# A hybrid decoder block on one core: 512-wide value rows, joined MoBA value products, gathers in every second expert pair, and an earlier overflow check

## The chip, the cores and the metric

The kernel runs on one NeuronCore of one Trainium2 chip, as one program that is launched once. The metric is the device time of an execution in microseconds (us), and a kernel's time is the median of its runs. TensorE (PE) multiplies matrices into PSUM, which has eight banks here; ScalarE (ACT), VectorE (DVE) and GpSimd (POOL) work on rows, and SyncE (SP) issues the DMAs.

## What is computed

One layer for 512 tokens of width 1024: a mixer with two branches, cross-attention into 256 memory rows, a mixture of experts, and a last RMSNorm. Cut to what matters here:

```python
def reference(x, mem, ...):
    x = x + mixer(rmsnorm(x, g_mix), ...)              # h @ w_in -> GLA q,k,v,... | MoBA q,k,v | gates
    x = x + memory_attention(rmsnorm(x, g_cross), ...) # 4 heads, 256 memory rows
    x = x + hier_moe(rmsnorm(x, g_moe), ...)           # top-1 of 4 groups, top-2 of its 8 experts
    return rmsnorm(x, g_final)

# MoBA, 8 heads of 64: softmax over the own block and chosen past blocks, then
#   out = p_own @ v_own + p_sel @ v_sel
# expert e on its tokens xb, with routing weight w:
#   hid = silu(xb @ w_gate[e]) * (xb @ w_up[e]);  y = (hid @ w_down[e]) * w
```

All numbers are float32. The gate, up and down weights of the 32 experts (1024x512, 1024x512 and 512x1024 each) are 201 MB of the 252 MB that the kernel moves.

## The kernel before, in words

**Front.** The weights of the projections, output and memory stages come through SP's queue as tiles of 512 KB (`wraw`). Each is split into a high and a low part (`wsplit`: ACT copies `whi`, DVE or POOL subtracts for `wlo`), and a product is three matmuls (`mm3`). Two forms exist: `in_feat` puts features on the partitions and has 512 tokens as columns (PSUM tile `fo`), and `in_rows` puts 128 tokens on the partitions and a strip of the weight's columns beside them (tiles `ro0` to `ro3`). `in_rows` makes the values: `vg` for GLA, `vm` for MoBA and `vc` for the memory, each in two passes of 256 columns. At the very start the rows of `x` are normalised (`rms_scale` squares them, by default on ACT, for `x_in[1]` on DVE), transposed and split (`to_feat`: `hTh` by ACT, `hTl` by DVE).

**MoBA.** For four head pairs (`hp`) and four query tiles (`i`) the kernel forms scores (`s_ps`), normalises them on DVE and ACT (`pr`), transposes them (`ptp`) into `pt`, and multiplies by the values (`mo_ps`). The program is software-pipelined by one item: the value products of an item stand behind the scores of the next one. Between the scores and the transposes of an item, `weave` puts matmuls of the gates (`fo`) as filling; how many is set by the table `FILL`.

**Experts.** Tokens are routed to 64 places (`CAP`) for each expert; two experts make a pair, and there are 16 pairs p = 0 to 15. A group is two pairs. `gather` collects the tokens of a group into `xT` by a product with one-hot rows (tile `g_ps`, eight steps); `gate_up` makes `gu_ps` in eight k steps; `hidden` and `hidden_t` give `hid_t` (tile `ht_ps`); `down` makes `y_ps`; `combine` adds a pair's result to `x` during the next pair (tile `c_ps`, eight steps). `c_bcast` (tile `cb_ps`, four steps) spreads codes and routing weights over the partitions before the first combination. Each pair needs 24 weight tiles of 512 KB (`we`), 16 for gate and up and 8 for down. `eload(n)` issues them in the order of use until n are issued: `DEPTH` tiles ahead of the pair's own first, `D0` for pair 0. All lie in a pool of 48 buffers that the front's tiles share, at most 8 DMAs are outstanding, and a DMA whose buffer isn't free holds SP's queue.

**Overflow.** An expert with more than 64 tokens is finished in a loop (`overflow`) whose count `n_extra` is read from the device (`values_load`, a TENSOR_LOAD on each engine). With these inputs it runs no turn: the page of the profile has 128 loads each of gate, up and down, no more than the pairs need. Every engine passes the loop's entry, and no `eload` past `elimit` is made ahead of it. The order within a pair is that of the code: gate and up, hidden, combine and gather steps, down.

Of the kernel before, what the change touches and what calls it, by code (L numbers as in the profile page):

```python
# [70 lines left out]
def block_kernel(ctx, tc, x, mem, g_mem, rel_bias, g_mix, w_in, w_alpha_up, b_alpha, g_gla_head, w_proj_gla,  # L71
# [94 lines left out]
    def chain(*gens):  # L166
        for g in gens:
            yield from g

# [20 lines left out]
    for j in range(2):  # L190
        add_rows(w_in, 512 + 256 * j, 256)
    add_feat(w_in, 2064, 4)
    add_feat(w_in, 1552, 4)
    for j in range(2):
        add_rows(w_in, 2576 + 256 * j, 256)
# [9 lines left out]
    for j in range(2):  # L205
        add_rows(w_ckv, 512 + 256 * j, 256)
# [152 lines left out]
    def in_rows(n, evac, src, nt=NT, mark=None):  # L359
        acc = [ps(f"ro{t}", [n]) for t in range(nt)]  # L360
        for kh in range(2):
            wh, wl = wnext(4, n)
            for t in range(nt):
                for k in range(4):
                    kk = 4 * kh + k
                    mm3(acc[t], src.hi[kk][:, tcol(t)], src.lo[kk][:, tcol(t)], wh[:, k, :], wl[:, k, :], kk == 0,
                        kk == KD - 1)
                    yield 0.33
                if kh:
                    evac(t, acc[t])  # L370
        marks.add(mark)
# [107 lines left out]
    def project():  # L479
        yield from in_feat(2, lambda i, o: S.activation(qk[2 + i], o, AF.Copy), hT)  # L480
        yield from in_feat(2, lambda i, o: S.activation(qk[i], o, AF.Copy, scale=0.125), hT, mark="qk")
        for j in range(2):
            yield from in_rows(256, lambda t, o: S.activation(vg[t][:, 256 * j:256 * j + 256], o, AF.Copy), hT)
        marks.add("v")
        yield from in_feat(4, keys, hT)
        yield from in_feat(4, queries, hT)
        vm.extend(rows2("vm", NT))
        for j in range(2):
            yield from in_rows(256, lambda t, o: S.activation(vm[t][:, 256 * j:256 * j + 256], o, AF.Copy), hT)
# [148 lines left out]
    def moba():  # L638
        def scores(hp, i):
            L = (i + 1) * P  # L640
            far = max(i - 1, 0) * P
            res = []
            for half in range(2):
                h = 2 * hp + half
                s_ps = ps("s_ps", [max(L, 256)])
                for part in range(2):
                    mm(s_ps, qmT[h][:, tcol(i)], kmT[h][part][:, 0:max(L, 256)], part == 0, part == 1)
                s_ps = s_ps[:, 0:L]
                pr = med("pr", [512])
# [24 lines left out]
        def transposed(i, res):  # L674
            pts = []
            for pr, _ in res:
# [5 lines left out]
                pts.append(pt)  # L682
            return pts

        def values(hp, i, pts, o_ps):
            for j in range(i + 1):
# [7 lines left out]
        prev, o_ps = None, {}  # L694

        def finish(hp, i, pts):
            if i == 0:
                o_ps[hp] = ps("mo_ps", [T])
            values(hp, i, pts, o_ps[hp])
            if i == NT - 1:  # L700
                split(om.hi[hp], om.lo[hp], o_ps[hp])

        for hp, i in items:
            res = scores(hp, i)
            if prev:
                finish(*prev)
            yield 0.64 * FILL[i][0]
            normalise(i, res)
            yield 0.64 * FILL[i][1]
            prev = hp, i, transposed(i, res)  # L710
        yield 1.0
        finish(*prev)
# [238 lines left out]
    eloads, elimit = [0], [12 * (NE - 2) + SPILL_AT]  # L951
# [128 lines left out]
    vgen = chain(*(in_rows(256, lambda t, o, j=j: S.activation(vc[:, t, 256 * j:256 * j + 256], o, AF.Copy), mn, nt=2)  # L1080
                   for j in range(2)))
# [4 lines left out]
    steps(vgen, 16)  # L1086
# [108 lines left out]
    def gather(oh, xT, ns):  # L1195

        for k in range(KD):
            o = ps("g_ps", [ns])
# [33 lines left out]
    def hidden_t(hid, n=P):  # L1232
        t_ps = ps("ht_ps", [4, n])
# [21 lines left out]
    def combine(ot, ys):  # L1255

        for t in range(NT):
            for c, y in ys.items():
                o = ps("c_ps", [512])
# [5 lines left out]
    def overflow(xi, xb):  # L1265
        n_extra = nc.values_load(xi[0:1, 0:1], min_val=0, max_val=NX - 1,
                                 skip_runtime_bounds_check_because="2 T assignments fill fewer than NX whole blocks")
        with tc.For_i(0, n_extra, 1, iteration_sync='staggered') as i:  # L1268
# [13 lines left out]
            drain(gather(oh, xT, CAP))  # L1282
            ot, ws = slot_rows(codes[0:CAP], CAP, oa)
            to = [blk("we", [2, 512]) for q in range(4)]
            gu, load = [ps("gu_ps", [512]) for q in range(2)], load_gate_up(bass.ds(e, 1), to)
# [4 lines left out]
            hid_t = hidden_t(hidden(gu, ws, CAP, hid), CAP)  # L1290
            y_ps, load = [ps("y_ps", [512]) for c in range(2)], load_down(bass.ds(e, 1), to)
# [3 lines left out]
            for c in range(2):  # L1295
                drain(combine(ot, {c: rows_hilo(y_ps[c], CAP, parts)}))

    NP = NE // 2
    bcast, slot, spill = c_bcast(), None, spill_list()
    comb, gat = iter(()), iter(())  # L1300
    xT_next = None
    for p in range(NP):
        w = blocks[2 * p:2 * p + 2]
        used = 24 * p
        if p == NP - 1:
            eload(elimit[0])
            overflow(*spilled)
            elimit[0] = 12 * NE
        eload(used + D0[0] if p == 0 else used + DEPTH)
# [4 lines left out]
        for k in range(KD):  # L1314
            gate_up(gu, k, [xT[k][:, s0 + CAP * i:s0 + CAP * i + CAP] for i in range(2)], w)
            if k % 2:
                eload(D0[1 + k // 2] if p == 0 else used + DEPTH + 2 * (k + 1))
            if p == 0 and k >= BC_AT:
                next(bcast, None)
                if k == BC_AT + 3:  # L1320
                    slot = slot_rows(sid[:, 0:1])
                    oh_next = group_hots(1)
        if p % 2 == 0 and p + 2 < NP:
# [13 lines left out]
        drain(comb)  # L1337
# [3 lines left out]
        if p % 2 and p + 3 < NP:  # L1341
            oh_next = group_hots((p + 3) // 2)
# [5 lines left out]
        for ft in range(4):  # L1348
            down(y_ps, hid_t, ft, w)
            eload(used + DEPTH + 16 + 2 * (ft + 1))  # L1350
# [34 lines left out]
    def finish(t, r):  # L1385
# [4 lines left out]
        SY.dma_start(out[tcol(t), 0:512], xg[t])  # L1390
# [21 lines left out]
SPILL_AT = 8  # L1412
# [8 lines left out]
DEPTH = 30  # L1421
D0 = 34, 37, 41, 44, 47
# [31 lines left out]
```

## Time and profile before

| | |
|---|---|
| median of 3 runs | 985.21 us (985.02 to 985.25) |
| the profiled execution | 985.1 us, its span 983.3 us |
| mean granted TensorE clock | 0.995 |
| PE busy | 961.1 us, 98% of the span |
| moved by DMA | 252.52 MB, mean 257 GB/s |

The span is what the trace covers; 1.8 us lie around it. A busy PE says little here: matmuls are pipelined, and an engine that executes one short matmul after the other is as busy as one at its peak. Stretches and gaps are read from the timeline, where a row is a run of like instructions, its first number the start and its second the time until the last of them ended. The trace counts an unsplit float32 matmul as two instructions, so a pair's gate and up products are 64 of them and its down products 32.

### The profile page before, as it was taken

What the parts mean: (1) busy time and instruction counts of PE and PEld (TensorE: products, weight loads), DVE (VectorE), ACT (ScalarE), POOL (GpSimd) and SP (SyncE); (2) the same over time, 40 slices, a digit from 0 to 9 for tenths busy, and PEclk for the clock granted to TensorE, in tenths of its full rate; (3) what the DMA queues carried; (4) which work ended last, traced back from release to release, by engine and by line L of the source; (5) the groups of instructions that cost most, each with busy time, mean ns of one, the idle gap of its engine ahead of it and who ended that gap; (6) DMA issues with size and microseconds to landing.
All of it is one profiled execution on the core that took longest, in us unless ns stands there. A gap on an engine that the chain in (4) does not pass through costs nothing. (4 is left out here: it accounts for less than half of the span.)

```text
span 983.3 us, 13899 instructions
## 1 busy us (share of the span) xinstructions
PE 961.1 (98%) x5305; PEld 645.5 (66%) x5305; DVE 474.8 (48%) x1048; ACT 311.7 (32%) x631; POOL 32.7 (3%) x46
## 2 busy tenths in 40 slices
PE   9999999999999999999999999999999999999985
PEld 7889779888788888999844555544555554455432
DVE  6343863345555746566752543434453333444314
ACT  5452633445446424455521111111111111111003
POOL 3200010000000000000000000000000000000003
PEclk9999999999999999999999999999999999999998
DMA  9512347133133522644588999999999999999993
GB/s 300 160 44 58 71 65 193 44 86 86 60 133 129 176 81 67 198 190 196 200 331 329 409 408 409 409 409 408 409 409 409 409 408 409 409 409 409 409 383 148
DMA packets 117161, 252.52 MB, mean 257 GB/s; under 512 B 10310, under 2 KB 61795, under 8 KB 117092
## 3 DMA queue, kind: packets, MB, share of 16 engines
q1 hardware_dynamic: 117092, 251.60, 69.3%
q8 instruction: 43, 0.70, 0.3%
q14 instruction: 26, 0.21, 0.1%
HBM read 247.90 MB, written 3.67 MB: 256 GB/s over the span
## 5 line engine op out<-in xcount | busy, mean ns | idle before, releaser
L136 PE MATMUL gu_ps<-we,xT 128*64 128x512 f32 x1024 | 229.3, 597 | 5.1 <-PEq L1268 3.8
L136 PEld LDWEIGHTS gu_ps<-we,xT 128*64 128x64 f32 x1024 | 78.0, 138 | 150.5 <-issue 134.6
L213 DVE TENSOR_TENSOR wlo<-wraw,whi 128x1024 fp32r<-128x1024 f32 (+1 forms) x71 | 86.6, 1238 | 90.0 <-ACT whi L212 89.8
L136 PE MATMUL y_ps<-we,hid_t 128*64 128x512 f32 x512 | 114.2, 595 | 0.3 <-issue 0.3
L1229 DVE SCALAR_TENSOR_TENSOR hid<-hid,ws,gu_ps 128x512 f32<-128x512 f32 x16 | 11.9, 747 | 194.9 <-PE gu_ps L136 194.9
L1262 DVE TENSOR_TENSOR x<-c_ps,x 128x512 f32<-128x512 f32 x120 | 76.7, 685 | 38.9 <-PE c_ps L136 38.9
L131 PE MATMUL fo<-hTh,whi 128*128 128x512 f32 x224 | 90.5, 404 | 0.0
L133 PE MATMUL fo<-hTh,wlo 128*128 128x512 f32 x224 | 87.5, 391 | 0.0
L132 PE MATMUL fo<-hTl,whi 128*128 128x512 f32 x224 | 87.4, 390 | 0.0
L136 PEld LDWEIGHTS y_ps<-we,hid_t 128*64 128x64 f32 x512 | 36.3, 137 | 68.8 <-issue 55.7
L212 ACT ACTIVATE whi<-wraw 128x1024 fp32r<-128x1024 f32 (+2 forms) x73 | 74.5, 1043 | 1.9 <-DMA wraw<-in_w_in_dram 1.8
L1228 ACT ACTIVATE hid<-gu_ps 128x512 f32<-128x512 f32 x16 | 9.6, 597 | 197.5 <-PE gu_ps L136 197.5
L136 PE MATMUL g_ps<-oh,xrh 128*128 128x256 f32 x256 | 64.6, 293 | 1.7 <-DVE oh L1030 1.7
L136 PE MATMUL g_ps<-oh,xrl 128*128 128x256 f32 x256 | 61.6, 281 | 0.0
L136 PEld LDWEIGHTS g_ps<-oh,xrh 128*128 128x128 f32 x256 | 47.0, 189 | 14.9 <-PE gu_ps L136 9.7
L133 PE MATMUL ro<-whi,hTl 128*128 128x256 f32 (+1 forms) x192 | 55.4, 289 | 0.8 <-DVE hTl L333 0.8
L131 PE MATMUL ro<-whi,hTh 128*128 128x256 f32 (+1 forms) x192 | 56.0, 291 | 0.0
L132 PE MATMUL ro<-wlo,hTh 128*128 128x256 f32 (+1 forms) x192 | 55.5, 289 | 0.2 <-POOL wlo L213 0.2
L212 ACT ACTIVATE yh<-y_ps 128x512 fp32r<-128x512 f32 x32 | 19.1, 598 | 109.9 <-PE y_ps L136 109.9
L136 PE MATMUL c_ps<-yh,ot 128*128 128x512 f32 x128 | 50.8, 397 | 0.7 <-ACT yh L212 0.7
L136 PE MATMUL c_ps<-yl,ot 128*128 128x512 f32 x128 | 50.8, 397 | 0.2 <-DVE yl L213 0.2
L131 PEld LDWEIGHTS fo<-hTh,whi 128*128 128x128 f32 x224 | 42.0, 188 | 12.0 <-issue 3.9
(320 smaller groups left out, 1544.5 us busy)
## 6 DMA issues: line engine op xcount, KB each, us to landing
we<-in_w_exp_gate_dram SPq DMA_DIRECT2D x128, 512.0 KB, 10.2
we<-in_w_exp_up_dram SPq DMA_DIRECT2D x128, 512.0 KB, 10.2
we<-in_w_exp_down_dram SPq DMA_DIRECT2D x128, 512.0 KB, 10.2
wraw<-in_w_in_dram SPq DMA_DIRECT2D x38, 512.0 KB, 3.8
wraw<-in_w_out_dram SPq DMA_DIRECT2D x8, 512.0 KB, 6.1
wraw<-in_w_ckv_dram SPq DMA_DIRECT2D x8, 512.0 KB, 4.6
wraw<-in_w_proj_gla_dram SPq DMA_DIRECT2D x4, 512.0 KB, 3.9
wraw<-in_w_proj_moba_dram SPq DMA_DIRECT2D x4, 512.0 KB, 4.3
```

The costliest lines, as they stand in the source:

```text
L131: PE.matmul(o, lh, rh, start=first, stop=False)
L132: PE.matmul(o, lh, rl, start=False, stop=False)
L133: PE.matmul(o, ll, rh, start=False, stop=last)
L136: PE.matmul(o, l, r, start=first, stop=last, **kw)
L212: S.activation(hi, src, AF.Copy)
L213: eng.tensor_tensor(lo, src, f(hi), op=ALU.subtract)
L1228: S.activation(row, gu[0][0:n], AF.Silu)
L1229: V.scalar_tensor_tensor(row, row, ws[:, 0:1], gu[1][0:n], op0=ALU.mult, op1=ALU.mult)
L1262: V.tensor_tensor(xs, o, xs, op=ALU.add)
```

## The change

1. `in_rows` makes 512 columns in one pass (two k rows to a weight tile, table `WIDE`), for `vg`, `vm` and `vc`.
2. MoBA: the transposes of a head pair's four query tiles are collected in `pa` and `pb`, copied by ACT in two pieces for tiles 2 and 3, and `values` runs once for a head pair, behind the scores of the next pair's first tile.
3. The square of `x_in[1]` is made on ACT, between the halves of `to_feat`.
4. The gather of a group stands wholly in the odd pair ahead of it (eight steps in pairs 1, 3, ... 13), not in halves in two pairs; pair 0 has none. Two of the four `c_bcast` steps stand ahead of `c_weights`. The prefetch depth is 35 tiles for pair 0 and 33 then, where it was 34 to 47 by a table and 30.
5. The overflow loop stands in pair 14 ahead of gate step k = 4, not ahead of pair 15; until there 350 tiles may be issued, not 368. Its count is loaded ahead of pair 13.
6. Four of the eight output DMAs are issued by ACT, not by SP.

```diff
-    def in_rows(n, evac, src, nt=NT, mark=None):
-        acc = [ps(f"ro{t}", [n]) for t in range(nt)]
-        for kh in range(2):
-            wh, wl = wnext(4, n)
+    def in_rows(evac, src, nt=NT, mark=None):
+        acc = [ps(f"ro{t}", [512]) for t in range(nt)]
+        kk = 0
+        for kn in WIDE:
+            wh, wl = wnext(kn, 512)
             for t in range(nt):
-                for k in range(4):
-                    kk = 4 * kh + k
-                    mm3(acc[t], src.hi[kk][:, tcol(t)], src.lo[kk][:, tcol(t)], wh[:, k, :], wl[:, k, :], kk == 0,
-                        kk == KD - 1)
-                    yield 0.33
+                for k in range(kk, kk + kn):
+                    mm3(acc[t], src.hi[k][:, tcol(t)], src.lo[k][:, tcol(t)], wh[:, k - kk, :], wl[:, k - kk, :], k == 0,
+                        k == KD - 1)
+                    yield 0.65
...
-    r1 = rms_scale(x_in[1], V)
-    to_feat(xr, hT, 0, lambda: wsplit(2))
-    rows[1] = scaled_rows(x_in[1], r1, gmix)
+    r1 = []
+    def between():
+        r1.append(rms_scale(x_in[1]))
+        wsplit(2)
+    to_feat(xr, hT, 0, between)
+    rows[1] = scaled_rows(x_in[1], r1[0], gmix)
...
-                pt = med("pt", [i + 1, P])
-                S.activation(pt, t_ps, AF.Copy)
+                n = min(i + 1, 2)
+                S.activation(pa[:, 0:n, tcol(i)], t_ps[:, 0:n, :], AF.Copy)
+                if i > 1:
+                    S.activation(pb[:, 0:i - 1, tcol(i - 2)], t_ps[:, 2:i + 1, :], AF.Copy)
...
-                    mm(o_ps[sl, tcol(i)], vm[j][:, h * 64:(h + 1) * 64], pts[half][:, j, :], j == 0, j == i,
-                       skip_group_check=True)
+                    p_j = pa[:, j, j * P:] if j < 2 else pb[:, j - 2, (j - 2) * P:]
+                    mm(o_ps[sl, j * P:], vm[j][:, h * 64:(h + 1) * 64], p_j, j == 0, j == NT - 1, skip_group_check=True)
...
-            if prev:
-                finish(*prev)
+            if prev and i == 0:
+                values(*prev)
...
-        if p == NP - 1:
-            eload(elimit[0])
-            overflow(*spilled)
-            elimit[0] = 12 * NE
-        eload(used + D0[0] if p == 0 else used + DEPTH)
+        depth = DEPTH[min(p, 1)]
+        if p == SPILL[0] - 1:
+            n_extra = nc.values_load(spilled[0][0:1, 0:1], ...)
+        eload(used + depth)
...
         for k in range(KD):
+            if (p, k) == SPILL[0:2]:
+                overflow(n_extra, *spilled)
+                elimit[0] = 12 * NE
             gate_up(gu, k, ...)
             if k % 2:
-                eload(D0[1 + k // 2] if p == 0 else used + DEPTH + 2 * (k + 1))
+                eload(used + depth + 2 * (k + 1))
...
-        if p % 2 == 0 and p + 2 < NP:
+        if p % 2 and p + 1 < NP:
             xT_next = rows2("xT", KD, 4 * CAP)
             gat = gather(oh_next, xT_next, 4 * CAP)
...
-        gs = 4 if p + 2 < NP else 0
-        steps(gat, min(gs, 1))
-        steps(comb, 2 if gs else 4)
+        steps(gat, 2)
+        steps(comb, 2 if p % 2 and p + 1 < NP else 4)
         hid_t = hidden_t(hid)
         for i in range(3):
-            steps(gat, min(gs, 1))
+            steps(gat, 2)
             steps(comb, 2)
...
-        SY.dma_start(out[tcol(t), 0:512], xg[t])
+        S.dma_start(out[tcol(t), 0:512], xg[t])
...
+WIDE = 2, 2, 2, 2
+SPILL = 14, 4, 350
-DEPTH = 30
-D0 = 34, 37, 41, 44, 47
+DEPTH = 35, 33
+OH_AT = 3
```

On PE, this is the passage from the first head pair of MoBA to the second in the program of before; `ptp` are the transposes of the last query tile, `s_ps` the scores of the next head pair's first tile, and `fo` the gates' filling:

```order
L679 MATMUL ptp<-keep,pr 128x128 x8
L136 MATMUL s_ps<-km_1092,qm_1412 128x256 x2
L136 MATMUL s_ps<-km_1093,qm_1412 128x256 x2
L136 MATMUL mo_ps<-pt,vm_1518 64x128 x4
L136 MATMUL mo_ps<-pt,vm_1519 64x128 x4
L131 MATMUL fo<-hTh_145,whi 128x512
```

and this is the same passage in the program of the change:

```order
L675 MATMUL ptp<-keep,pr 128x128 x8
L136 MATMUL s_ps<-km_989,qm_1309 128x256 x2
L136 MATMUL s_ps<-km_990,qm_1309 128x256 x2
L136 MATMUL mo_ps<-pa,vm_1415 64x512 x2
L136 MATMUL mo_ps<-pa,vm_1415 64x384 x2
L136 MATMUL mo_ps<-pb,vm_1416 64x256 x2
L136 MATMUL mo_ps<-pb,vm_1416 64x128 x2
L131 MATMUL fo<-hTh_145,whi 128x512
```

Eight products of 128 columns, for one query tile, have become eight of 512 to 128 columns, for all four; the products that stood behind the three scores between are gone.

On SP, this is the entry of the overflow loop in the program of before; the DMAs ahead of it are the first tiles of pair 15, `rt_xi` holds the loop's count, and the branch is the loop's:

```order
L940 DMA we<-in_w_exp_gate_dram 128x1024
L940 DMA we<-in_w_exp_up_dram 128x1024
L1266 TENSOR_LOAD rt_xi
L1268 COMPARE_AND_BRANCH
```

and this the same place in the program of the change, where the DMAs are among the last tiles of pair 14's gate and up weights:

```order
L935 DMA we<-in_w_exp_gate_dram 128x1024
L1301 TENSOR_LOAD rt_xi
L935 DMA we<-in_w_exp_up_dram 128x1024
L935 DMA we<-in_w_exp_gate_dram 128x1024
L935 DMA we<-in_w_exp_up_dram 128x1024
L935 DMA we<-in_w_exp_gate_dram 128x1024
L935 DMA we<-in_w_exp_up_dram 128x1024
L1262 COMPARE_AND_BRANCH
```

The load of the count stands five DMAs ahead of the branch now. On PE it stands a whole pair ahead. The branch there follows the down products of pair 14 in the program of before:

```order
L136 MATMUL y_ps<-we,hid_t 64x512 x16
L1266 TENSOR_LOAD rt_xi
L1268 COMPARE_AND_BRANCH
```

and in the program of the change it parts the gate and up products of pair 14 (32 in this count) in halves:

```order
L136 MATMUL y_ps<-we,hid_t 64x512 x16
L136 MATMUL gu_ps<-we,xT_7449 64x512 x16
L1262 COMPARE_AND_BRANCH
```

What stands directly ahead of the branch on PE is no longer work whose result DVE and ACT have yet to take out of PSUM for the combination.

## Rows read from the trace of the kernel before

**Rows 1.** Page, parts 1, 2 and 6.

```profile
PE 961.1 (98%) x5305; PEld 645.5 (66%) x5305; DVE 474.8 (48%) x1048; ACT 311.7 (32%) x631; POOL 32.7 (3%) x46
...
GB/s 300 160 44 58 71 65 193 44 86 86 60 133 129 176 81 67 198 190 196 200 331 329 409 408 409 409 409 408 409 409 409 409 408 409 409 409 409 409 383 148
...
wraw<-in_w_in_dram SPq DMA_DIRECT2D x38, 512.0 KB, 3.8
```

**Rows 2.** Windows: length, busy of PE, PEld, DVE, ACT, POOL, clock, DMA share, GB/s.

```profile
500.00:520.00 20.00, 19.52 (x97) 7.89 (x98) 9.79 (x26) 6.27 (x12) 0.00 (x0) 1.00 0.94 349
520.00:540.00 20.00, 20.00 (x103) 8.19 (x103) 3.12 (x8) 2.83 (x6) 0.00 (x0) 1.00 0.84 322
540.00:880.00 340.00, 339.74 (x1746) 167.02 (x1744) 145.10 (x297) 51.54 (x96) 0.00 (x0) 1.00 1.03 409
908.00:940.00 32.00, 27.58 (x124) 11.37 (x122) 11.04 (x20) 2.99 (x5) 0.00 (x0) 1.00 1.00 396
941.00:943.00 2.00, 2.00 (x6) 0.60 (x4) 0.00 (x0) 0.00 (x0) 0.00 (x0) 0.50 1.04 404
```

**Rows 3.** Timeline of PE and SP, pair 0 and pair 1.

```profile
499.89 5.37 PE L136 MATMUL gu_ps<-we,xT 128*64 128x512 f32 x24
...
507.77 16.89 SPq L946 DMA_DIRECT2D we<-in_w_exp_down_dram  x8
...
512.54 0.65 PE L1073 MATMUL cb_ps<-keep,rt_wts 128*128 128x128 f32 x4
...
522.38 7.09 PE L136 MATMUL y_ps<-we,hid_t 128*64 128x512 f32 x32
...
529.29 13.90 PE L136 MATMUL gu_ps<-we,xT 128*64 128x512 f32 x64
...
551.28 7.09 PE L136 MATMUL y_ps<-we,hid_t 128*64 128x512 f32 x32
```

**Rows 4.** Timeline of PE, pairs 13 to 15.

```profile
888.84 1.08 PE L136 MATMUL gu_ps<-we,xT 128*64 128x512 f32 x4 [0.35 <-DMA we<-in_w_exp_gate_dram]
...
923.67 0.50 PE L136 MATMUL c_ps<-yh,ot 128*128 128x512 f32 x1
...
928.01 7.09 PE L136 MATMUL y_ps<-we,hid_t 128*64 128x512 f32 x32
938.86 16.50 PE L136 MATMUL gu_ps<-we,xT 128*64 128x512 f32 x64 [3.77 <-PEq L1268]
...
959.63 5.98 PE L136 MATMUL y_ps<-we,hid_t 128*64 128x512 f32 x24
```

**Rows 5.** Timeline of SP and DVE, the overflow loop and the outputs.

```profile
931.21 0.33 SPq L940 DMA_DIRECT2D we<-in_w_exp_up_dram  x1
...
935.92 0.69 DVE L213 TENSOR_TENSOR yl<-y_ps,yh 128x512 fp32r<-128x512 f32 x1 [0.29 <-ACT yh L212]
...
938.72 0.33 SPq L940 DMA_DIRECT2D we<-in_w_exp_gate_dram  x1
...
979.34 0.61 SPq L1390 DMA_DIRECT2D out_dram<-xg  x1
```

**Rows 6.** Windows of tiles `ro` and `fo`: PE, PEld, DVE, ACT busy, clock, DMA.

```profile
79.77:90.09 10.32, 10.32 (x88) 10.27 (x86) 0.00 (x0) 1.15 (x3) 1.00 0.19 51
...
96.33:102.23 5.90, 5.90 (x28) 4.88 (x26) 0.00 (x0) 1.25 (x3) 1.00 0.30 89
```

**Rows 7.** Windows of tile `mo_ps`, one head pair of MoBA; the same columns.

```profile
182.00:210.00 28.00, 3.51 (x40) 2.30 (x40) 0.00 (x0) 0.55 (x1) 1.00 0.28 76
```

**Rows 8.** Timeline of DVE and PE, MoBA's last query tile of a head pair.

```profile
205.47 0.49 DVE L672 TENSOR_SCALAR pr<-pr,ri 128x512 f32<-128x512 f32 x1
...
205.86 0.60 PE L679 MATMUL ptp<-keep,pr 128*128 128x128 f32 x4
```

**Rows 9.** Timeline of all engines, the start.

```profile
9.16 1.70 DVE L300 CUSTOM_DVE_ANT_0 junk<-xi 128x1024 f32<-128x1024 f32 x1 [1.45 <-DMA xi<-in_x_dram]
...
11.26 0.59 PE L133 MATMUL ro<-whi,hTl 128*128 128x272 f32 x1 [0.83 <-DVE hTl L333]
```

More of the change, by code (lines that the diff above doesn't have):

```diff
@@ L189, in block_kernel @@
     add_feat(w_in, 0, 2)
-    for j in range(2):
-        add_rows(w_in, 512 + 256 * j, 256)
+    add_rows(w_in, 512, 512, WIDE)
     add_feat(w_in, 2064, 4)
     add_feat(w_in, 1552, 4)
-    for j in range(2):
-        add_rows(w_in, 2576 + 256 * j, 256)
+    add_rows(w_in, 2576, 512, WIDE)
     add_feat(w_in, 3088, 16)
@@ L204, in block_kernel @@
     add_feat(w_cq, 0, 4)
-    for j in range(2):
-        add_rows(w_ckv, 512 + 256 * j, 256)
+    add_rows(w_ckv, 512, 512, WIDE)
     for c in range(2):
@@ L481, in project @@
         yield from in_feat(2, lambda i, o: S.activation(qk[i], o, AF.Copy, scale=0.125), hT, mark="qk")
-        for j in range(2):
-            yield from in_rows(256, lambda t, o: S.activation(vg[t][:, 256 * j:256 * j + 256], o, AF.Copy), hT)
-        marks.add("v")
+        yield from in_rows(lambda t, o: S.activation(vg[t], o, AF.Copy), hT, mark="v")
         yield from in_feat(4, keys, hT)
@@ L487, in project @@
         vm.extend(rows2("vm", NT))
-        for j in range(2):
-            yield from in_rows(256, lambda t, o: S.activation(vm[t][:, 256 * j:256 * j + 256], o, AF.Copy), hT)
+        yield from in_rows(lambda t, o: S.activation(vm[t], o, AF.Copy), hT)
     gla_out = []
@@ L672, in normalise, with transposed @@
                 V.tensor_scalar(pr[:, 0:(i + 1) * P], pr[:, 0:(i + 1) * P], ri, None, op0=ALU.mult)
-        def transposed(i, res):
-            pts = []
-            for pr, _ in res:
+        def transposed(i, res, pts):
+            for (pr, _), (pa, pb) in zip(res, pts):
                 t_ps = ps("ptp", [i + 1, P])
@@ L679, in transposed, with values @@
                     PE.transpose(t_ps[:, j, :], pr[:, tcol(j)], ident)
-                pt = med("pt", [i + 1, P])
-                S.activation(pt, t_ps, AF.Copy)
[L682 to L686, printed above, removed]
+                n = min(i + 1, 2)
+                S.activation(pa[:, 0:n, tcol(i)], t_ps[:, 0:n, :], AF.Copy)
+                if i > 1:
+                    S.activation(pb[:, 0:i - 1, tcol(i - 2)], t_ps[:, 2:i + 1, :], AF.Copy)
+        def values(hp, pts):
+            o_ps = ps("mo_ps", [T])
+            for j in range(NT):
                 for half in range(2):
@@ L709, in moba @@
             yield 0.64 * FILL[i][1]
-            prev = hp, i, transposed(i, res)
+            if i == 0:
+                prev = hp, [(blk("pa", [2, T]), med("pb", [2, 2 * P])) for half in range(2)]
+            transposed(i, res, prev[1])
         yield 1.0
-        finish(*prev)
+        values(*prev)
     fill = gates()
@@ L950, in block_kernel @@
     blocks = [[] for _ in range(NE)]
[L951 removed]
+    eloads, elimit = [0], [SPILL[2]]
     def load_pairs():
@@ L1078, in block_kernel @@
     xT = rows2("xT", KD, 4 * CAP)
-    vgen = chain(*(in_rows(256, lambda t, o, j=j: S.activation(vc[:, t, 256 * j:256 * j + 256], o, AF.Copy), mn, nt=2)
-                   for j in range(2)))
+    vgen = in_rows(lambda t, o: S.activation(vc[:, t, :], o, AF.Copy), mn, nt=2)
     c_scores(0)
@@ L1085, in block_kernel @@
     c_exp(1)
-    steps(vgen, 16)
+    steps(vgen, 8)
     c_normalise(0)
@@ L1143, in block_kernel @@
         c_gather_part(NT - 1, kk, 0)
+    bcast = c_bcast()
+    steps(bcast, 2)
     c_weights()
@@ L1193, in group_hots, with gather @@
         return oh
-    def gather(oh, xT, ns):
+    def gather(oh, xT, ns, to=None):
         for k in range(KD):
-            o = ps("g_ps", [ns])
+            o = to[k % 2] if to else ps("g_ps", [ns])
             for t in range(NT):
@@ L1230, in hidden, with hidden_t @@
         return hid
-    def hidden_t(hid, n=P):
-        t_ps = ps("ht_ps", [4, n])
+    def hidden_t(hid, n=P, t_ps=None):
+        t_ps = ps("ht_ps", [4, n]) if t_ps is None else t_ps
         for a in range(4):
@@ L1253, in product, with combine @@
             mm(o, ot[:, tcol(t)], y[i], first and i == 0, i == 1)
-    def combine(ot, ys):
+    def combine(ot, ys, to=None):
         for t in range(NT):
             for c, y in ys.items():
-                o = ps("c_ps", [512])
+                o = to[t] if to else ps("c_ps", [512])
                 product(o, ot, t, y)
@@ L1263, in combine, with overflow @@
                 yield t, c
-    def overflow(xi, xb):
-        n_extra = nc.values_load(xi[0:1, 0:1], min_val=0, max_val=NX - 1,
-                                 skip_runtime_bounds_check_because="2 T assignments fill fewer than NX whole blocks")
+    def overflow(n_extra, xi, xb):
         with tc.For_i(0, n_extra, 1, iteration_sync='staggered') as i:
@@ L1281, in overflow @@
                 tile_hots(oh, rel, t, CAP, part)
-            drain(gather(oh, xT, CAP))
+            pb = [ps("sp_ps", [512]) for q in range(6)]
+            drain(gather(oh, xT, CAP, [b[:, 0:CAP] for b in pb[0:2]]))
             ot, ws = slot_rows(codes[0:CAP], CAP, oa)
             to = [blk("we", [2, 512]) for q in range(4)]
-            gu, load = [ps("gu_ps", [512]) for q in range(2)], load_gate_up(bass.ds(e, 1), to)
+            gu, load = pb[2:4], load_gate_up(bass.ds(e, 1), to)
             for j in range(4):
@@ L1289, in overflow @@
                     gate_up(gu, k, xT[k:k + 1], [{2 * j + q: w[q] for q in range(2)}])
-            hid_t = hidden_t(hidden(gu, ws, CAP, hid), CAP)
-            y_ps, load = [ps("y_ps", [512]) for c in range(2)], load_down(bass.ds(e, 1), to)
+            hid_t = hidden_t(hidden(gu, ws, CAP, hid), CAP, pb[4][:, 0:4 * CAP].rearrange("p (a n) -> p a n", a=4))
+            y_ps, load = pb[0:2], load_down(bass.ds(e, 1), to)
             for ft in range(4):
@@ L1295, in overflow @@
             for c in range(2):
-                drain(combine(ot, {c: rows_hilo(y_ps[c], CAP, parts)}))
+                drain(combine(ot, {c: rows_hilo(y_ps[c], CAP, parts)}, pb[2:6]))
     NP = NE // 2
-    bcast, slot, spill = c_bcast(), None, spill_list()
+    slot, spill = None, spill_list()
     comb, gat = iter(()), iter(())
-    xT_next = None
     for p in range(NP):
@@ L1349, in block_kernel @@
             down(y_ps, hid_t, ft, w)
-            eload(used + DEPTH + 16 + 2 * (ft + 1))
+            eload(used + depth + 16 + 2 * (ft + 1))
         ys = {c: rows_hilo(y_ps[c]) for c in range(2)}
```

28 lines of the change are left out of this document (11 added, 17 removed).

## The prediction

> **What bounds the kernel now.** I read the page first. PE is busy for 961.1 of 983.3 us [rows 1], which here only says that it always has a matmul in flight. The line of GB/s in the same group tells more: from the middle of the span on it stands at 408 to 409, against some 40 to 300 in the front. The windows sharpen it: for 340 us, from 540 to 880, the stream of expert weights runs at 409 GB/s with a DMA share of 1.03 while PE has no gaps [rows 2]. Both are full, so the two rates must be compared. A tile of 524,288 bytes takes 1.28 us at 409 GB/s, and a pair's 24 tiles take 30.7 us. A pair on PE takes 28.9: its gate and up products start at 529.29, its down products at 551.28, and these last 6.91 (522.38 to 529.29, one pair before) [rows 3]. The stream is slower than PE by 1.8 us a pair, and the prefetched lead pays for it. Near the end the lead is used up: gate products wait for a tile at 888.84 [rows 4]. So in the experts' stage time is won where **the stream** loses it, and lost where the stream stands still; in the front, where DMA is far from full, time is won on PE and the chains that hold it.
>
> Where does the stream lose time? In pair 0: 349 GB/s from 500 to 520 and 322 from 520 to 540 [rows 2] are 20 x (1 - 349/409) + 20 x (1 - 322/409) = 2.9 + 4.3 = **7.2 us of standing**. The timeline of SP shows why: its down tiles stand in the queue from 507.77 for 16.89 us [rows 3], until the first down product of pair 0 (522.38) frees a buffer. And at the overflow loop: SP issues nothing from 931.21 to 938.72 [rows 5] and PE stands for 3.77 [rows 4]; since up to eight tiles were still on their way the stream itself lost little, 32 x (1 - 396/409) = 1.0 us [rows 2].
>
> **Value rows.** In a stretch of `ro` 86 products of 256 columns start in 10.32 us, 0.120 each; in one of `fo`, with the same split operands and 512 columns, 26 in 5.90, 0.227 each [rows 6]. vg and vm have 384 products of 256 columns and vc 96. 480 x 0.120 = 57.6 becomes 240 x 0.227 = 54.5: **-3.1 us**. The bounds: nothing, if 512 columns cost twice 0.120; -5.8, if they ran at the pace of the down products, 6.91/32 = 0.216 [rows 3]. I take `fo`, which has the same form. A weight tile holds two k rows of 512 columns in place of four of 256 and stays at 512 KB, so the loads and splits of the front keep their number and order; the halved number of evacuations lies beside PE's work.
>
> The Trainium skill (TensorE: Matmul & The Clock Gate, Back-to-back issue gap) gives an isolated product N/2.4 + 2.5 ns; by an estimate from that, two of 256 cost 218 ns and one of 512 cost 216, and this part would bring 0.6 us. The row for `ro` is 11 ns above the page's figure for 256 columns, the row for `fo` 11 ns above that for 512, so the trace bears out a fixed cost per instruction that the formula doesn't have.
>
> **MoBA.** One head pair's value products keep PE busy for 3.51 us in 40 instructions [rows 7]. The new ones are 16, with 512, 384, 256 and 128 columns four times each: at 0.216 for 512 that is 4 x 2.5 x 0.216 = 2.2. On PE alone it would bring 1.3 per head pair, 5.4 in all. But the products that vanish stood where PE waits for the softmax: for the last query tile DVE ends the second half's normalisation at 205.96, and PE begins to transpose the first half at 205.86 [rows 8]. There is no slack; what is removed ahead of such a transpose turns into a wait, since `FILL` puts in no more filling. And behind the scores of the next head pair the products get longer, and their last operand is now the third of four ACT copies. Bounds 0 and -5.4; I take the lower third, **-1.5**.
>
> **Start.** DVE's square of x_in[1] takes 1.70 us from 9.16, and PE's first product with `hTl` waits 0.83 for DVE [rows 9]. On ACT the square stands ahead of the next weight split, which is needed too. **-0.7**, between -1.4 (the wait and the one like it that follows) and +0.3.
>
> **`c_bcast`.** A step is four matmuls, 0.65 with its tail [rows 3], 0.6 net. Two steps ahead of pair 0 cost **+1.2** there, with nothing that hides them; pair 0 is shorter by as much, which is counted next.
>
> **Experts.** Pair 0 loses the gathers and two `c_bcast` steps. Its gate and up products take 13.85 + 1.2; then PE waits about 2.4 for `hidden` and `hidden_t`, which the gathers covered. The first down product comes 17.5 us after the stage's start, against 22.5 (499.89 to 522.38 [rows 3]): 5.0 earlier. Two more tiles fit ahead of it (the depth is 33 where it was near 31 when the queue stopped), 2.6 us more. 7.6 covers the 7.2 of standing: the stream runs through.
>
> The gathers themselves don't vanish: a pair with four steps takes 28.9 - 13.85 - 6.91 = 8.1 between its products, pair 14 without any 4.34 (923.67 to 928.01 [rows 4]), so a step costs 0.95, 56 of them as before. The odd pair gets longer by 3.8, the even one shorter; with a lead of 33 tiles (42 us of stream) neither starves.
>
> At the new loop PE arrives after 24.9 us of pair 0, 13 x 28.9 + 3.8 and half the gate products of pair 14, 6.9: 411.3 behind the stage's start. The stream may go to tile 350. Before, tile 368 was issued at 931.21; 18 x 1.28 earlier is 908.2, less the 7.2 that no longer stand: 401.0 behind the start, and the eight on their way land by 411.2. So the stream is dry just as PE arrives. The wait at the loop is what I know least. Of the 3.77, some 1.5 went until DVE had emptied PSUM (it ends at 936.61 [rows 5]) and the rest for the count and the branch; now PSUM is empty long before, the count is loaded a pair ahead, but all engines still meet. I take 1.5, from 0.5 to 3.8. Behind the branch stand, on PE, the rest of pair 14's gate products, which need tiles from 344 on, and on SP the last 34 tiles. The first tile behind it lands after 3.8 us [rows 1], 2.5 beyond its own 1.28. With 1.0 for the crossing of the two that is **5 us of standing**, from 3 to 7.3.
>
> Before, the last 16 tiles landed by 938.72 + 2.5 + 16 x 1.28 = 961.7 [rows 5], 461.8 behind the stage's start, and the first half of pair 15's down products ended at 959.63 + 3.6 [rows 4], 463.3 behind it. Now the last tile lands at 461.8 - 7.2 - 1.0 + 5 = 458.6, and the products that need it end 1.1 later, at 459.7: **-3.6**, from -5.6 to -1.3.
>
> **Outputs.** SP issues the last of eight outputs at 979.34 for 0.61 [rows 5]. ACT takes half of the issues, but the transfers share what moves them: **-0.4**, from 0 to -1.2. The Trainium skill (DMA: Bandwidth & Descriptors, Issuing engines are not separate DMA queues) says that other issuers save only the issue's time; the size of the row agrees.
>
> **Sum.** -3.1 - 1.5 - 0.7 + 1.2 - 3.6 - 0.4 = -8.1. The profiled execution took 985.1, 0.1 below the median shown: 985.2 - 8.1 = **977.1 us**. Its own range, by the middle of the bounds, is 974.5 to 979.5.
>
> **Rivals.** *The loop costs what it cost*: 3.77 in the middle of a pair. Against it speaks that DVE's part is gone; for it, that the rest is unexplained. The stream stands 2.3 longer, and if the clock falls to 0.50 (1.2 GHz) as it did behind the old wait (941 to 943 [rows 2]) PE loses another 1 to 2: 979.4 to 981.4. *MoBA pays on PE in full*, if the chains have more slack elsewhere than at the tile that I read: 3.9 better, 973.2. *Width saves nothing beyond columns*, the page's rule, as a mechanism here a floor set by columns alone: 0.6 in place of 3.1, 979.6; the two paces in rows 6 speak against it. *Slower*: an odd pair now pushes eight gather steps and eight combine steps through PSUM in 11.9 us, and DVE and ACT must empty both. If each odd pair is longer by x, PE comes to the loop 7x later while the stream stands dry: from x = 1.2 the gain is gone, at 1.5 the time is 987.6. Against it: DVE is busy for 145 of 340 us there [rows 2]. *No effect that shows*: the front's gains sink in chains and the loop costs 7: about 984.
>
> **How the numbers follow.** Chances: forecast 0.47, dear loop 0.18, full MoBA 0.12, width saves little 0.08, slower 0.08, no effect 0.07. A measurement can tell about 0.2% here, 2.0 us. The first four are faster by more than that, 0.85; same 0.07; slower 0.08. The range takes in all but the last two: from 972.0 (full MoBA with a cheap loop) to 982.5 (the dear loop with a poor start).
>
> **What would show it.** Right: `ro` at 0.227; MoBA's stretch with waits of PE for DVE or ACT ahead of transposes; no dip of GB/s in pair 0, one at pair 14's loop; gate or down products behind the loop that wait for tiles. Wrong: a dip in pair 0 still there; PE waits in odd pairs for g_ps or c_ps banks; a loop that costs nothing, or a low clock behind it.

## The result, and the profile after

The changed kernel took 995.68 us (median of 6 runs, 992.05 to 997.9), the kernel before 985.52 in the same series (985.02 to 986.52): a ratio of 1.0098, with a 95% interval from 1.0075 to 1.012. It is 10 us slower, where 8 us faster was forecast, and 13 us above the upper end of the range, 982.5. The profiled execution took 997.3, with a span of 995.5 and a mean granted clock of 0.987.

The page after has, for the lines of [rows 1], PE's busy time and the rate of the DMAs over the span in 40 slices:

```profile
PE 961.4 (97%) x4969; PEld 632.4 (64%) x4969; DVE 472.2 (47%) x1047; ACT 311.3 (31%) x639; POOL 32.6 (3%) x46
...
GB/s 303 151 44 63 69 74 176 64 64 85 64 191 127 190 22 142 160 277 94 292 399 409 361 409 406 409 409 410 409 409 409 409 408 409 408 409 186 267 409 148
```

PE is as busy as before, with 336 matmuls fewer. In the experts' stage the stream now has its deepest hole near the end (186, 267) and a small one early (361). The timeline of PE says what came before each:

```profile
493.24 5.37 PE L136 MATMUL gu_ps<-we,xT 128*64 128x512 f32 x24 [0.35 <-ACT xT L1042]
...
510.93 7.09 PE L136 MATMUL y_ps<-we,hid_t 128*64 128x512 f32 x32 [0.69 <-ACT hid_t L1233]
517.85 13.90 PE L136 MATMUL gu_ps<-we,xT 128*64 128x512 f32 x64
...
547.28 7.09 PE L136 MATMUL y_ps<-we,hid_t 128*64 128x512 f32 x32
...
572.46 7.09 PE L136 MATMUL y_ps<-we,hid_t 128*64 128x512 f32 x32
579.38 13.90 PE L136 MATMUL gu_ps<-we,xT 128*64 128x512 f32 x64
...
886.47 13.90 PE L136 MATMUL gu_ps<-we,xT 128*64 128x512 f32 x64
912.28 7.09 PE L136 MATMUL y_ps<-we,hid_t 128*64 128x512 f32 x32
...
926.75 5.33 PE L136 MATMUL gu_ps<-we,xT 128*64 128x512 f32 x22 [0.51 <-PEq L1262]
```

Set beside [rows 3] and [rows 4], three things stand here. The experts' stage starts at 493.24, not 499.89: the front gained 6.65 us. Pair 0's down products come 17.7 behind that start (22.5 before). And in pair 1 there are 547.28 - 517.85 - 13.85 = **15.6 us** between gate and down products, in pair 13 886.47 to 912.28 less 13.85, **12.0**. The pairs 3, 5, 7, 9 and 11 have 15.6 as well. 6 x 3.6 = 21.7 us, and so PE comes to the loop 433 us behind the stage's start, not 411. What stretches such a pair is seen in pair 3, in the timeline of all engines:

```profile
594.52 0.48 ACT L1198 ACTIVATE xT<-g_ps,gfeat 128x256 f32<-128x256 f32 x1 [1.43 <-PE g_ps L136]
...
598.70 0.48 ACT L1198 ACTIVATE xT<-g_ps,gfeat 128x256 f32<-128x256 f32 x1 [0.48 <-PE g_ps L136]
...
601.57 0.40 PE L136 MATMUL c_ps<-yl,ot 128*128 128x512 f32 x1
602.00 0.69 DVE L1258 TENSOR_TENSOR x<-c_ps,x 128x512 f32<-128x512 f32 x1 [1.54 <-PE c_ps L136]
602.75 0.50 PE L136 MATMUL c_ps<-yh,ot 128*128 128x512 f32 x1 [0.78 <-DVE x L1258]
...
603.52 0.69 DVE L1258 TENSOR_TENSOR x<-c_ps,x 128x512 f32<-128x512 f32 x1 [0.82 <-PE c_ps L136]
604.26 0.53 PE L136 MATMUL g_ps<-oh,xrh 128*128 128x256 f32 x1 [0.78 <-DVE x L1258]
...
607.37 0.41 PE L136 MATMUL g_ps<-oh,xrh 128*128 128x256 f32 x1
...
607.99 1.21 ACT L1198 ACTIVATE xT<-g_ps,gfeat 128x256 f32<-128x256 f32 x3 [8.81 <-PE g_ps L136]
```

Twice PE waits until DVE has read out the product that PE made just before. DVE isn't late: it starts 0.43 after that product's start, and it had been idle for 1.54. That is how a combine step would behave that has been given its forerunner's bank; a trace has no bank numbers, and the next section takes this up. ACT, too, stands still for 8.81 us, with two finished gather steps before it, and goes on only behind the last gather product; then it empties all four one behind the other. The last two gather steps then run at 0.213 us a product in place of 0.120; the windows of PE give the clock (the last three columns are clock, DMA share, GB/s):

```profile
592.00:600.00 8.00, 8.00 (x55) 1.00 1.03 410
...
604.20:607.80 3.60, 3.54 (x17) 0.53 1.02 407
```

Each of the two waits costs 0.95 (the product behind it starts 1.18 behind its forerunner, where the others start 0.23 apart), and 16 products cost 0.09 more each, 1.5 together: that is 3.4 of the 3.6. A granted clock of 0.53 means 1.2 GHz, in place of 2.4, for nearly all of that stretch, right behind the two waits.

The stream's standing, by the way of the prediction (length x (1 - rate/409)), from windows of the stage in the same columns:

```profile
493.00:513.00 20.00, 18.14 (x86) 1.00 0.93 357
513.00:533.00 20.00, 20.00 (x99) 1.00 1.03 410
533.00:553.00 20.00, 18.43 (x104) 0.91 0.91 357
900.00:915.00 15.00, 15.00 (x100) 1.00 0.50 198
915.00:930.00 15.00, 14.49 (x70) 1.00 0.16 46
930.00:945.00 15.00, 13.29 (x58) 1.00 0.97 377
```

That is 2.5 in pair 0, 2.5 in pair 1 and 22.2 at the loop, 27.2 in all. In pair 1 SP issues nothing from 540.04 to 549.24, until the late down products (from 547.28) free a buffer. SP shows the last, too: it reaches tile 350 and stops, and goes on when PE has come.

```profile
899.22 0.33 SPq L935 DMA_DIRECT2D we<-in_w_exp_up_dram  x1
926.76 0.33 SPq L935 DMA_DIRECT2D we<-in_w_exp_gate_dram  x1
```

### The profile page after: what moved, and what is told of

The parts are those of the page before. It is cut to its first block, busy times and chain, and to the rows that moved or that the text cites. A ratio compares the mean times of both kernels' runs of the same rounds, so it can differ in the third digit from the quotient of the medians.

```text
span 995.5 us, 13241 instructions
## 1 busy us (share of the span) xinstructions
PE 961.4 (97%) x4969; PEld 632.4 (64%) x4969; DVE 472.2 (47%) x1047; ACT 311.3 (31%) x639; POOL 32.6 (3%) x46
## 5 line engine op out<-in xcount | busy, mean ns | idle before, releaser
L136 PE MATMUL gu_ps<-we,xT 128*64 128x512 f32 x1024 | 226.4, 593 | 6.3 <-DMA we<-in_w_exp_gate_dram 3.2
L136 PEld LDWEIGHTS gu_ps<-we,xT 128*64 128x64 f32 x1024 | 74.2, 137 | 153.8 <-issue 132.6
L136 PE MATMUL g_ps<-oh,xrh 128*128 128x256 f32 x256 | 70.7, 315 | 6.1 <-DVE x L1258 4.7
L136 PE MATMUL g_ps<-oh,xrl 128*128 128x256 f32 x256 | 68.8, 307 | 0.0
L136 PEld LDWEIGHTS g_ps<-oh,xrh 128*128 128x128 f32 x256 | 53.3, 213 | 15.0 <-issue 7.3
L136 PE MATMUL c_ps<-yh,ot 128*128 128x512 f32 x128 | 52.9, 413 | 5.4 <-DVE x L1258 4.7
L136 PEld LDWEIGHTS g_ps<-oh,xrl 128*128 128x128 f32 x256 | 53.9, 216 | 0.4
L1198 ACT ACTIVATE xT<-g_ps,gfeat 128x256 f32<-128x256 f32 x56 | 24.7, 476 | 75.0 <-PE g_ps L136 57.5
L133 PEld LDWEIGHTS fo<-hTh,wlo 128*128 128x128 f32 x224 | 42.0, 188 | 9.1
```

The lines of the kernel that those rows point to most:

```text
L133: PE.matmul(o, ll, rh, start=False, stop=last)
L136: PE.matmul(o, l, r, start=first, stop=last, **kw)
```

## The experiments

Each is compared with the kernel before on the same chip. All keep the whole computation. "Odd pairs" are pairs 1, 3 ... 13, and their stretch is the time from the last gate product to the first down product.

**Depth 32** (`e1_depth32`), in the changed kernel:

```diff
-DEPTH = 35, 33
+DEPTH = 35, 32
```

My first theory came from how the built program gives out SBUF: in pairs 1 to 11 of the changed kernel the second half of the new `xT` gets the buffer of the one-hot tile that the gather is still reading, so ACT has to wait for the last gather product. With depth 32 it gets another.

> One number of the change is altered: the prefetch depth from pair 1 on is 32 tiles, not 33. Theory A (a buffer is short): the second half of xT gets the buffer of the very one-hot tile that the gather still reads, so ACT can empty no g_ps bank of the last four steps before the last gather product, PE runs out of banks, waits and loses its clock, 3.6 us in each of pairs 1, 3, 5, 7, 9, 11. With one tile less ahead, a buffer is free: the stretch between gate and down products of these pairs is 12.0 us as it is in pair 13 already (15.6 now), PE reaches the loop 21.7 us earlier, the stream stands about 5 us there, and the time is about 974 us. Theory B (eight gather and eight combine steps in one pair are too much for PSUM and its readers, whatever the buffers): the stretch stays at 15 to 16 us and the time at 993 to 998.

994.41 us, ratio 1.0088 (1.0057 to 1.012): no better than the change. The timeline of all engines in pair 3:

```profile
599.29 0.47 ACT L1198 ACTIVATE xT<-g_ps,gfeat 128x256 f32<-128x256 f32 x1 [1.40 <-PE g_ps L136]
...
601.46 0.50 PE L136 MATMUL c_ps<-yh,ot 128*128 128x512 f32 x1 [0.78 <-DVE x L1258]
...
602.97 0.39 PE L136 MATMUL g_ps<-oh,xrh 128*128 128x256 f32 x1 [0.78 <-DVE x L1258]
...
606.02 7.09 PE L136 MATMUL y_ps<-we,hid_t 128*64 128x512 f32 x32
```

ACT now empties the fifth step at once, so its long wait is gone, and yet PE's two waits are there. The stretch fell to 14.1 us in pairs 1 and 3 and stayed 15.6 in the four behind them, where the clock fell again. So ACT's wait was not the cause; theory A in that form fell. I then looked at which PSUM bank the built program gives to each tile (this stands in no trace). In both programs, in each of the odd pairs 1 to 11, three tiles in a row (two of `c_ps` and one of `g_ps`) have one and the same bank; in the kernel before and in pair 13 of the changed one no two neighbours do. That fits the two waits one by one.

**368 tiles ahead of the loop** (`e2_limit368`; `e4_d32_limit368` with depth 32 as well), and **the loop back ahead of pair 15** (`e3_d32_loop_as_before`, with depth 32):

```diff
-SPILL = 14, 4, 350
+SPILL = 14, 4, 368     # e2, e4
+SPILL = 15, 0, 368     # e3
```

> Depth 33 as in the change, but 368 tiles may be issued ahead of the overflow loop, not 350. Theory A: the odd pairs keep their 15.6 us and PE comes to the loop as late as now (433 us behind the stage's start), but the stream no longer stands there for 19 us; what follows the loop runs at PE's pace, 40 us to the first half of pair 15's down products, and the time is about 988 to 989. If the loop's own tiles lack buffers with 18 more tiles ahead, PE waits at the loop for more than 1 us and the time stays above 992.

> Depth 32, and the loop back ahead of pair 15 with 368 tiles ahead of it, as in the kernel before. Theory A and a dear loop: the odd pairs take 12.0 us, the loop costs PE about 3.8 us and a low clock behind it 1 to 2 more, the stream doesn't stand; about 971 to 973. If the earlier loop with its limit of 350 is worth something by itself, this run is slower than the one with depth 32 alone (974 expected); I expect it 1 to 3 us faster. Theory B: 985 or more.

> Depth 32 and 368 tiles ahead of the loop, which stays in pair 14 ahead of k = 4. Theory A: odd pairs of 12.0 us, a loop that costs PE 0.5 to 1.5 us, and no standing stream: about 969 to 971, the fastest of the four. If the standing of the stream is caused by the loop itself and not by the limit, it equals the run with depth 32 alone. Theory B: 985 or more.

996.11 (ratio 1.01, 1.0082 to 1.0117), 996.93 (1.0123, 1.0102 to 1.0143) and 996.23 us (1.0114, 1.0097 to 1.0131). None helps while the odd pairs are long; e2 ends above 992 with more than 1 us at the loop, as the second branch of its expectation has it, but that a lack of buffers is the reason is not shown. With 368 tiles pair 13 is stretched to 15.6 in all three as well, and in all three built programs it has its three tiles on one bank now. e2 differs from the changed kernel in the limit alone, with the gather where it was and the same depth; its pair 13 in the timeline of PE (887.13 to 916.55 less 13.85, against 12.0 above):

```profile
887.13 13.90 PE L136 MATMUL gu_ps<-we,xT 128*64 128x512 f32 x64
916.55 7.09 PE L136 MATMUL y_ps<-we,hid_t 128*64 128x512 f32 x32
```

PE waits 3.2 to 3.5 at the loop, not 0.51. In e3, where PE comes to the loop a pair later, the stream stands once more: from 915 to 960 it loses 21.6 us, most of it here:

```profile
930.00:945.00 15.00, 15.00 (x72) 6.67 (x68) 8.36 (x16) 1.58 (x3) 0.00 (x0) 1.00 0.02 8
```

In e2 and e4 it loses 5.4 and 3.1 between 915 and 945, and pair 15's gate products wait for no tile. So there the limit only moves the loss: PE, which is 21 to 25 us late, sets the end.

**The gather in halves again** (`e5_gather_halves`), in the changed kernel, cut:

```diff
-        if p % 2 and p + 1 < NP:
+        if p % 2 == 0 and p + 2 < NP:
             xT_next = rows2("xT", KD, 4 * CAP)
...
-        steps(gat, 2)
-        steps(comb, 2 if p % 2 and p + 1 < NP else 4)
+        gs = 4 if p + 2 < NP else 0
+        steps(gat, min(gs, 1))
+        steps(comb, 2 if gs else 4)
...
-            steps(gat, 2)
+            steps(gat, min(gs, 1))
...
-DEPTH = 35, 33
+DEPTH = 31, 31
```

> One part undone: the gather stands in halves in two pairs as in the kernel before (four steps in each of pairs 0 to 13), with a prefetch depth of 31 for all pairs, since deeper ones leave no buffers for it in pair 0. All else as changed. Theory C (the gather's place alone causes the loss, by PSUM banks that the program hands out again at once: in pairs 1 to 11 of the changed kernel three tiles in a row get one bank; here none do): pairs take 28.9 us again, pair 0 loses most of the stream that the change saves, and the time is about 979 us. Theory D (something else in the stage slows the odd pairs: the depth, the loop, the count loaded early): 990 or more.

**976.19 us** (975.55 to 976.38), ratio 0.9903 (0.9886 to 0.9919): 9 us faster than before, with everything of the change kept but the gather's place and the depth. Theory C stands on the place of the gather. D falls for the loop and the count, which are as changed; the depth, which went to 31 with the gather, this run does not part from it. In its windows (columns as above) the stream stands 3.9 + 0.9 in pair 0 and 0.7 at the loop:

```profile
493.00:513.00 20.00, 19.75 (x108) 1.00 0.91 330
513.00:533.00 20.00, 20.00 (x96) 1.00 1.01 391
...
900.00:915.00 15.00, 12.47 (x59) 1.00 0.99 390
```

**Two sets of xT** (`e6_two_xt_sets`), the gather whole in the odd pair as changed; `e7_two_xt_sets_368` has 368 tiles ahead of the loop in addition:

```diff
-    xT = rows2("xT", KD, 4 * CAP)
+    xTs = [rows2("xT", KD, 4 * CAP) for q in range(2)]
+    xT = xTs[1]
...
-            xT_next = rows2("xT", KD, 4 * CAP)
+            xT_next = xTs[(p // 2) % 2]
...
-DEPTH = 35, 33
+DEPTH = 35, 31
```

> The gather stays whole in the odd pair, but xT has two sets of buffers that are held for good, in place of new ones from the pool that the weight tiles fill; depth 35 and 31. In this program three tiles in a row share one bank in pair 1 alone, not in pairs 1 to 11. Theory C1 (the pool's shortage of buffers for xT made the program hand out the banks badly): the stretch between gate and down products is 12.0 us in pairs 3 to 13 and 14 to 15.6 in pair 1, and the time is about 975 to 978. Theory C2 (eight gather and eight combine steps in one pair overload PSUM whatever the buffers): the stretch stays 14 us or more in all odd pairs and the time above 988.

983.82 us, ratio 0.9982 (0.9972 to 0.9992). C1 is right on the stretch: it is 12.0 in pair 3 (579.48 to 605.29 less 13.85) and in the odd pairs behind it (from the last gate product on; in pairs 11 and 13 some of these wait for tiles), and 15.6 in pair 1, the one pair where the program still puts three tiles on a bank. But the time is 6 us over what I expected. The timeline of PE, and the windows:

```profile
579.48 13.90 PE L136 MATMUL gu_ps<-we,xT 128*64 128x512 f32 x64
...
605.29 7.09 PE L136 MATMUL y_ps<-we,hid_t 128*64 128x512 f32 x32
```

```profile
493.00:513.00 20.00, 18.06 (x86) 1.00 0.94 355
...
533.00:553.00 20.00, 18.43 (x104) 0.91 0.79 307
900.00:915.00 15.00, 14.50 (x70) 1.00 0.70 275
915.00:930.00 15.00, 13.61 (x60) 1.00 0.97 362
```

The stream stands 2.6 in pair 0, 5.0 in pair 1 and 4.9 + 1.7 at the loop, 14.2. The 5.0 I had not foreseen: the tiles that follow wait for buffers that pair 1's down products free, and these come late when the gathers and the waits stand ahead of them. The row of SP in which it waits 10.8 us for a down product:

```profile
529.64 20.01 SPq L941 DMA_DIRECT2D we<-in_w_exp_down_dram  x8
```

> As the run with two xT sets, but 368 tiles may be issued ahead of the loop. If the limit of 350 makes the stream stand about 5 us at the loop, this is 2 to 4 us faster, about 972 to 974. If the loop's wait on PE grows with it (3.48 us was seen with depth 32 and 368, 0.81 with 350), the gain is 1 us or less.

995.86 us, ratio 1.0111 (1.0089 to 1.0132): 12 slower than e6, neither of the two that I gave. PE and SP at the loop:

```profile
923.09 0.33 SPq L935 DMA_DIRECT2D we<-in_w_exp_up_dram  x1
931.40 0.33 SPq L935 DMA_DIRECT2D we<-in_w_exp_gate_dram  x1
```

```profile
931.45 8.56 PE L136 MATMUL gu_ps<-we,xT 128*64 128x512 f32 x32 [20.66 <-PEq L1263]
```

PE comes in time, at 910.8, and waits 20.66 us. The loop stands on SP's queue behind the 368th tile, which is issued at 923.09, and PE goes on with SP's next issue. What holds both for the 8.3 us between stays open. So the limit cuts both ways: too low, and the stream stands while PE comes; too high, and PE stands while SP issues. With 350 the stream stands 0.7 us at the loop in e5, where PE comes 413 behind the stage's start, and 6.6 in e6, where it comes at 419.

**Parts of the front alone**, in the kernel before: MoBA's joined products (`e8_moba_alone`), the 512-wide rows (`e9_wide_alone`), the square on ACT (`e10_square_alone`); each is its part of the diff of the change.

> The kernel before with the joined value products of MoBA alone. My prediction took 1.5 us for this part, since I read no slack in the softmax chain; that gives 983.7. The trace of the changed kernel says that the stretch from the first to the last scores is 4.8 us shorter (116.9 to 112.1), which gives 980.4 if it reaches the end.

> The kernel before with the 512-wide value rows alone. My term: 480 products at 0.120 us become 240 at 0.227, -3.1 us, about 982.2. The rival from the Trainium skill's formula (TensorE: Matmul & The Clock Gate, Back-to-back issue gap) is -0.6, about 984.7. The traces of the two kernels show the stage's start earlier by 1.2 for vg, 1.2 for vm and 0.4 to 0.6 for vc; I hold to 982.2 to 982.6.

> The kernel before with the square of x_in[1] on ACT alone. My term was -0.7; by the trace of the changed kernel the last hTl at the start is 0.3 us earlier and the first product of GLA's state 1.5, of which 1.2 is vg. So -0.3, about 985.0, which can't be told from no change; -0.7 would be 984.6, and a delay of the weight splits by ACT 985.5 or more.

981.28 us (ratio 0.9957, 0.9943 to 0.9971), 982.89 (0.9976, 0.9965 to 0.9986) and 984.47 (0.9993, 0.9983 to 1.0002). In their profiled executions the experts' stage starts at 495.43, 497.02 and 499.89, so MoBA is worth 4.5 there, the rows 2.9, the square nothing. With the two `c_bcast` steps (0.8 in the trace after, from 490.90 to the next product at 491.69) that makes 6.5 of the 6.65.

**Two more with the gather in halves**: the loop as before (`e11_halves_loop_as_before`, `SPILL = 15, 0, 368`) and pair 0's depths as before (`e12_halves_deep_pair0`, the table `D0` of before).

> The run with the gather in halves (depth 31, 976.2 us), and in addition the loop back ahead of pair 15 with 368 tiles ahead of it. The stream stood 4.8 us in pair 0 and 0.7 at the loop there. By the accounting of the stream, the kernel before stood 1.0 at its loop, so the loop's place is worth less than 1 us as long as the stream sets the end: 976 to 977. If the wait on PE counts (3.8 and a low clock behind it against 2.5), it is 978 to 980.

> The run with the gather in halves, and in addition the table of depths for pair 0 of the kernel before (34, 37, 41, 44, 47 in place of 31 to 39). If the stream's 4.8 us of standing in pair 0 come from the shallow depth there, 3 or more of them vanish and the time is 972 to 974, the best so far. If buffers set it, whatever the table says, it stays at 976.

976.54 (0.9911, 0.9895 to 0.9928) and 976.22 us (0.9909, 0.9893 to 0.9926), both as e5. The loop's new place is worth nothing by itself here. The table does not set pair 0's standing; in e5 and in e12 SP waits the same 5.9 us there for a down product, which frees a buffer.

## Why the prediction was wrong

**The step that failed** is "The odd pair gets longer by 3.8, the even one shorter; with a lead of 33 tiles neither starves." The 3.8 is right: pair 13 has 12.0 us, 8.1 + 3.8. What the step left out, and so put at nothing, is that the odd pairs 1 to 11 would lose 3.6 more each to PSUM. I had it as the rival "slower", with x = 1.2 as the point from which the gain is gone, and gave it 0.08. x came out at 3.6, in six of the seven. My ground against it, DVE busy for 145 of 340 us [rows 2], says nothing on this: neither reader was overloaded (DVE idle for 1.54 ahead of the read that PE waits for). A bank was given out again at once. The order of the instructions and [rows 2] don't tell that; the numbers of the banks in the built program do, and I did not look at them. e5 shows that the gather's place is what costs, e6 that buffers for `xT` change the banks and with them the stretch. e6 has depth 31 as well; the program with depth 31 and `xT` from the pool has the three tiles in all six pairs too, but it was not run. The cleanest pair of runs is e2 against the changed kernel, where pair 13 goes from 12.0 to 15.6 with its banks and no step of the pair is altered. The stream runs on beside it in e2, but so it does beside pair 3 of e6, which takes 12.0. In all the programs that were run with a whole gather, each odd pair with three tiles on a bank takes 14.1 or 15.6 and each other one 12.0. Why the program's builder puts three tiles on a bank in one program and not in the other is open.

**Then the loop** turned a late PE into a standing stream. The prediction has the stream dry "just as PE arrives", 411; PE came at 433, and the stream had been dry for 17 us by then (3 GB/s from 909.5 to 926.75). The terms join: 977.1 + 21.7, less 2.5 by which the front was better than forecast, is 996.3; the profiled execution took 997.3 and the median is 995.7. The 5.0 of standing in pairs 0 and 1, which no term has, do not come on top: they put the issue of tile 350 at 406.0 behind the start (899.22), where 401.0 was forecast, and the stream stands so much less at the loop. The 24.9 for pair 0 in the forecast of PE's arrival is a slip (its own terms give 17.5 + 6.9 = 24.4) that changes nothing.

**The stream as what bounds the stage** was right where PE keeps up or waits for it, and it accounts for four kernels; it does not for e2, e4 and e7, where PE, late or held at the loop, sets the end. Against e5 (975.6 in its profiled execution, stage from 493.25, 5.5 us of standing):

| | start later by | standing more by | together | time more by |
|---|---|---|---|---|
| before | 6.6 | 8.2 - 5.5 = 2.7 | 9.3 | 9.5 |
| changed | 0 | 27.2 - 5.5 = 21.7 | 21.7 | 21.7 |
| e6 | 0.1 | 14.2 - 5.5 = 8.7 | 8.8 | 8.5 |

**The terms.** *Value rows*: -3.1 forecast, 2.9 earlier at the stage's start in e9 and -2.3 in its median (interval -3.4 to -1.4). The 0.6 from the Trainium skill's formula (TensorE: Matmul & The Clock Gate, Back-to-back issue gap) lies outside that: the paces of [rows 6] decided. *MoBA*: -1.5 forecast, -4.1 measured (interval -5.6 to -2.9); the rival "MoBA pays on PE in full" was right, at a smaller price than its 5.4. The window of [rows 7] after the change:

```profile
182.00:210.00 28.00, 2.44 (x16) 1.50 (x16) 0.69 (x1) 0.60 (x1) 1.00 0.21 57
```

That is 2.44 a head pair, where 2.2 was forecast, so PE saves 1.1 in each and 4.3 in all, about what was measured. "There is no slack" was a misreading. I set the end of DVE's *second* half (205.96) beside PE's transposes of the *first* (205.86) in [rows 8]. The first half's normalisation is the row one normalisation earlier in the timeline of DVE before:

```profile
204.69 0.49 DVE L672 TENSOR_SCALAR pr<-pr,ri 128x512 f32<-128x512 f32 x1
```

It ends at 205.18, 0.68 ahead of PE. After the change the same place shows the slack used up, and waits of 0.34 and 0.16 beyond it:

```profile
201.84 0.63 PE L675 MATMUL ptp<-keep,pr 128*128 128x128 f32 x4 [0.34 <-DVE sm L666]
202.62 0.63 PE L675 MATMUL ptp<-keep,pr 128*128 128x128 f32 x4 [0.16 <-DVE pr L669]
```

*Start*: -0.7 forecast; e10 can't be told from no change. *`c_bcast`*: +1.2, found 0.8. *Pair 0*: the first down product 17.7 behind the start, 17.5 forecast; the stream still stood 2.5 there, where none was forecast. *The loop's wait on PE*: 1.5 forecast. At the new place it was 0.5 to 0.8 where the stream was dry (the changed kernel, e1, e6), 2.5 to 3.5 where it ran (e2, e4, e5, e12), and 20.66 in e7; at the old place it was 3.2 in e3, with the stream dry, and 3.1 in e11. What sets this is open. *Outputs*: -0.4 forecast; no run has them alone, but from the start of the last down product to the end of the span it is 14.4 us before (from 968.9) and after (from 981.1), so nothing of it is seen.

## What to carry to other kernels

When products are moved together into one stretch, look at which PSUM bank each tile gets in the built program: two neighbours on one bank put the reader's latency on PE, however idle the reader is, and a change far from the products (here the buffers of `xT`, or how many tiles may be issued ahead of a loop) can change the banks. Where two full rates meet, add up the slower one's standing time, as long as the faster one keeps up; here it told the times of three kernels against a fourth to within 0.3 us. Slack is read half by half, each result against the instruction that takes it.

## What the runs showed of the hardware

Two waits of 0.78 us, 1.5 apart, cost the clock in some pairs and not in others of the same kernel. In the run with depth 32 they stand at the same places in pair 3 (601.46 and 602.97) and pair 5; the windows behind them (PE busy, clock, DMA share, GB/s):

```profile
604.00:606.00 2.00, 2.00 (x14) 1.00 1.02 408
...
663.00:667.40 4.40, 4.40 (x20) 0.61 1.05 415
```

The first stayed at 2.4 GHz, the second ran most of its length at 1.2, and that is 1.5 us of the stretch (14.1 and 15.6). Ahead of the experts' stage of the changed kernel a single wait of 1.40 left the clock alone:

```profile
489.88 1.19 PE L136 MATMUL g_ps<-oh,xrh 128*128 128x256 f32 x8 [1.40 <-DVE oh L1025]
```

```profile
490.00:493.00 3.00, 2.89 (x24) 1.00 0.08 34
```

The Trainium skill (TensorE: Matmul & The Clock Gate, What's actually happening) calls throttling the default state, which activity releases. These rows agree in so far as the clock fell only behind waits; the length of the waits alone does not tell when.
